# Operands of both token sets beside the classic gate slices, an own bank for some last products, and a later second mixture split

## The chip, the cores and the metric

The kernel runs on one core of a Trainium2 chip. The metric is the device time of one execution in microseconds, as the median of several runs. The profile is that of one further execution, whose own time stands beside its span below. The engines are TensorE (PE in the profile; its weight loads are PEld), VectorE (DVE), ScalarE (ACT), GpSimd (POOL) and SyncE (SP); SP and POOL issue most of the transfers.

## The reference, cut to what matters

One decoder layer for 1024 prompt tokens and 8 sample tokens that share the weights (1032 tokens, model width 1024, feed-forward width 2816), all in float32:

```python
h = rmsnorm(x, g_attn_norm)
z = h @ w_in                       # q, k, v of both branches, mLSTM gates, merge gates A and M
y_a = sliding_window_attention(...) @ w_att_out
y_m = mlstm_chunkwise(...) @ w_mlstm_out
mixed = sigmoid(gate_a) * y_a + sigmoid(gate_m) * y_m
x = x + mixed @ w_out
h2 = rmsnorm(x, g_ffn_norm)
x = x + (silu(h2 @ w_gate) * (h2 @ w_up)) @ w_down
y = rmsnorm(x, g_final)
```

It also returns the key and value windows and the mLSTM states. gate_a and gate_m are 1024 columns each of `w_in`.

## The kernel before

**Number format.** Every large product is made of three float32r matmuls. Each operand x is split into a high part (an ACT copy to float32r) and a low part (VectorE: x minus the high part), and a product is low weights by high activations, high weights by low activations, and high by high. So each operand costs one ACT and one VectorE instruction before TensorE can use it.

**Classic slices and products of seven.** Part of the matrix products are done in the classic way, one weight slice of 128 columns after the other (`Slice`, `gemm`). The others, called visits, use Winograd's form of Strassen's scheme: a two by two block product with 7 instead of 8 block products. The weights of a visit form four blocks, from which four sums S1 to S4 are made (`weight_sum`, on VectorE); the activations form four blocks b11, b12, b21, b22, which are turned into sums t1 to t4 once for all visits and split into high (`gh` in the gate stage, `Th` in the feed-forward) and low (`gl`, `Tl`) operands. The tokens are cut into two halves of 516, and each half into two sets of 258. An operand of the activations belongs to one set.

**A visit.** `product(n, sets)` issues product n, for n = 0, 2, 1, 4, 3, 5, 6 in this order. For one set and four blocks of rows in the contraction it is 12 matmuls of 128 by 258. Three PSUM tiles of two banks each are used: product 2 goes to `b`, products 4 and 6 to `d`, and 0, 1, 3 and 5 all go to `a`, one added on top of the other. After each of them ACT copies the state of `a` (p1 after 0, U2 after 1, V after 3), and the next product into `a` has to wait for that copy. Product 6 adds on top of what product 4 left in `d`. `after(n, sets)` gives the work that follows a product: `now` is issued with this step, `later` with the next. Where a visit does both sets at once (24 matmuls a product) product 0 of the next visit stands between products 3 and 5. The first gate visit and the first up visit do set 0 alone and then set 1; for set 0, and in the last visit of a chain, nothing stands between 3 and 5.

**Stages in order of time.** Classic slices up to attention and the mLSTM; four classic gate slices m0, a0, m1, a1 (`gate_tile`, three chunks of 344 tokens each, 12 jobs); six gate visits `GV` (columns 2 to 7); the two branch projections (`branch_tile`, wm and wa); the output projection in 16 tiles (`wo_tile`, 8 for set 0, then 8 for set 1); 22 up visits `UP`; 20 down visits `DOWN`; a classic rest of the down projection and the final norm.

**What runs beside the classic gate slices.** After each of the 12 jobs one entry of the list `gate_work` is issued (`gate_plan`): the rest of the head gate, block sums and operands of set 0 (`GateBlocks(0)`, B0), the weight operands of the first gate visit (`p(0)`, `p(2)`, `p(1)`, `p(4, 3)`) and those of set 1 (B1). Each job's own evacuation, the sigmoid `sg` (L1071), is issued on ACT before that job's entry and behind those of all earlier jobs. The weight operands 0 and 4 use the buffers `wh`, 2 and 3 the buffers `wl`, two of each, which the classic slices use too. What the list leaves is attached to the first steps of the first visit (`first_hooks`, `hk[-1]`, `hk[0]` and so on: hooks of the step of that number).

**What sets the order.** TensorE, SP and POOL run in program order (`IN_ORDER`). ACT and VectorE run in program order for everything issued through `main_line`; other instructions are placed by a scheduler when their inputs are ready. `side.step` lets side jobs (generators) go on beside an output tile: 6 steps for each `wo_tile`, two more at its start. The side jobs of the output stage are the first 6 steps of `residual()` (the transposes of the input rows), then `mix_rest()` (the split of the mixture for set 1), then the rest of `residual()`. `next_split` splits the weight slice that comes two tiles later; in `run` it is issued after a tile's matmuls and before its evacuation.

**Buffers.** `up` has 20 buffers of 1032 columns (U), `tp` 11 smaller ones (T), `vp` 18. PSUM has 8 banks: six are the three two-bank tiles (`ps_d`), in the earlier stages six single ones (`ps_g`, `ps_a`), and two are `ps_t`, for transposes and small sums.

Of the kernel before, what the change touches and what calls it, by code (L numbers as in the profile page):

```python
# [35 lines left out]
HB = 258  # L36
# [48 lines left out]
def decoder_step(ctx, tc, x_prompt, x_sample, cache_k, cache_v, st_c, st_n, st_m, rel_bias, w_in, b_if, sinks,  # L85
# [204 lines left out]


    class Tile:
        def __init__(self, prods, evac, per=0.0, before=None, pre=None, mm=None, after=None):
            self.prods, self.evac, self.per, self.before, self.pre, self.mm, self.after = prods, evac, per, before, pre, mm, after

# [36 lines left out]
    def run(tiles, jobs, sl, loads, splits):  # L332
# [10 lines left out]
        for n, (t, c) in enumerate(jobs):  # L343
            tile_ = tiles[t]
            if t not in started:
                started.add(t)
                if tile_.before:
                    tile_.before()
            if tile_.pre:
                tile_.pre(c)  # L350
            rate = tile_.per / sum(len(rhs) for _, rhs in tile_.prods)

            def tick():
                acc[0] += rate
                if acc[0] >= 1.0 - 1e-9:
                    acc[0] -= 1.0
                    side.step(1)

            pss = []
            for i, (w, rhs) in enumerate(tile_.prods):  # L360
                if tile_.mm:
                    ps = tile_.mm(w, tick)
                else:
                    ps = ps_g(f"{w.name}_{c}")
                    gemm(ps, w.w, rhs, slice(*CHUNKS[c]), tick)
                pss.append(ps)
                if last[t] == n and splits and not w.own:
                    next_split()
            main_line(tile_.evac, c, *pss)
            if tile_.after:  # L370
                tile_.after()
            if n + 2 < FIRST and len(sl) > FIRST and not mark:
                sl[n + 2].split()
            if n + 1 == START and not mark:
                mark.append(len(nc.cur_bb.bb.instructions))
# [827 lines left out]

    def mix_rest():
        for th in range(2):
            for k in range(0, KD, 4):
                mix_split(1, th, range(k, k + 4))
                yield

    d_x1 = [dp.tile([P, NT], F32, name=f"d_x1_{j}") for j in range(KD)]  # L1210
# [174 lines left out]

    ngate = len(tiles)
    tiles.extend(branch_tile(n, j) for n in "ma" for j in range(KD))
    tiles.extend(wo_tile(s, j) for s in range(2) for j in range(KD))


# [100 lines left out]
    class Visit:  # L1491
# [40 lines left out]
                self.ops[n] = o  # L1532

        def view(self, t, sets):
            return t[:, sets[0]:sets[-1] + 1, 0:HB]

        def small(self, name, sets):
            return T(f"{name}{self.name}_{sets[0]}", [P, len(sets), HB])

        def product(self, n, sets):  # L1540
            bank = "b" if n == 2 else "d" if n in (4, 6) else "a"
            first = n in (0, 2, 4)
            if first:
                self.box[bank] = ps_d(f"{bank}{self.name}_{sets[0]}")
            ps, o = self.box[bank], self.ops[n]
            for s in sets:
                for k in range(self.nk):
                    hi, lo = self.act(n, s, k)
                    for i, (a, b) in enumerate(((o[:, 1, k], hi), (o[:, 0, k], lo), (o[:, 0, k], hi))):
                        pe.matmul(ps[:, s, 0:HB], a, b, start=(first and k == 0 and i == 0), stop=(k == self.nk - 1 and i == 2),  # L1550
                                  skip_group_check=not first)

    def prep_rest():
# [4 lines left out]
    class UpVisit(Visit):  # L1558
# [16 lines left out]
        def after(self, n, sets):  # L1575
# [22 lines left out]
                later.append(c22)  # L1598
            elif n == 5:
                box["s2"] = self.small("s2", sets)  # L1600
                now.append(lambda: act.activation(box["s2"], get("a"), AF.Silu))
                later.append(lambda: tt(dve, box["uu"][:, 1, s0:s1], box["uu"][:, 1, s0:s1], box["s2"], ALU.mult))
            elif n == 6:
                u1 = box["uu"][:, 0, s0:s1]
# [7 lines left out]
    class GateVisit(Visit):  # L1612
# [16 lines left out]
        def after(self, n, sets):  # L1629
# [16 lines left out]
            elif n == 3:  # L1646
                box["V"] = self.small("V", sets)
                now.append(lambda: act.copy(box["V"], get("a")))
# [17 lines left out]
    class DownVisit(Visit):  # L1666
# [21 lines left out]
        def after(self, n, sets):  # L1688
# [12 lines left out]
            elif n == 3:  # L1701
                box["V"] = self.small("V", sets)
                now.append(lambda: act.copy(box["V"], get("a")))
# [501 lines left out]
```

## Time and profile before

| what | value |
|---|---|
| median of 3 runs | 1424.61 us (1424.02 to 1426.32) |
| the profiled execution's own time | 1427.2 us |
| its span | 1425.2 us, 26898 instructions |
| PE busy | 1388.3 us (97%) |
| DVE busy | 909.4 us (64%) |
| ACT busy | 620.6 us (44%) |
| POOL busy | 139.5 us (10%) |
| granted TensorE clock, mean | 0.99 |

A row of the timeline holds the start, the duration, the engine, the line and the operation, and what it writes and reads; in square brackets the idle time of the engine before it and what ended it. Successive matmuls overlap, so a matmul that shows 0.28 us follows the last after 0.12. A row of waits holds who waited for whom, the sum, the number and the longest. Names of tiles are cut: ag, bg, dg are the PSUM tiles of the gate visits, af, bf, df those of the up visits, ad, bd, dd those of the down visits, and op0 to op6 the weight operands. Line L124 is the helper for all two-operand VectorE instructions.

### The profile page before, as it was taken

The page shows a single profiled execution, that of the slowest core. Times are in us where ns is not written, and L with a number is a line of the kernel's source. Part 1 is how long each engine was busy: PE and PEld are TensorE (multiplying, and loading weights), DVE is VectorE, ACT ScalarE, POOL GpSimd, SP SyncE. Part 2 cuts the span into 40 slices and gives each one's busy share as a digit, 9 for nine tenths or more (in the row PEclk, how much of TensorE's full clock was granted, in tenths as well). Part 3 has the DMA queues.
Part 4 walks back from the last instruction along what each step waited for, and adds up shares of the span by engine and source line. Part 5 has one row for each costly group of instructions (what it writes and reads, how often), then busy time and mean ns, then how long its engine had stood idle before and what let it go on. Part 6 is the DMA issues. An engine that isn't in the chain of part 4 may idle for free.

```text
span 1425.2 us, 26898 instructions
## 1 busy us (share of the span) xinstructions
PE 1388.3 (97%) x10723; PEld 1350.7 (95%) x10724; DVE 909.4 (64%) x1827; ACT 620.6 (44%) x1403; POOL 139.5 (10%) x240
## 2 busy tenths in 40 slices
PE   8999999999879999999999999999999999999996
PEld 7998888999879999999999999999999999999996
DVE  7252657784664444653776666766666668888875
ACT  6243477654343332354453444434343433333324
POOL 4011011001110110000110111111001100000003
PEclk9999999999989999999999999999999999999999
DMA  7144214013323255588531444443344467777633
GB/s 218 32 126 98 67 55 97 16 60 121 97 77 108 90 215 179 159 287 294 188 104 53 156 164 165 152 146 119 123 132 149 164 202 274 228 249 233 215 119 119
DMA packets 179172, 208.41 MB, mean 146 GB/s; under 512 B 20638, under 2 KB 137634, under 8 KB 179032
## 3 DMA queue, kind: packets, MB, share of 16 engines
q1 hardware_dynamic: 161928, 151.72, 34.8%
q0 software_dynamic: 16688, 54.40, 10.3%
q8 instruction: 84, 1.38, 0.4%
q10 hardware_dynamic: 432, 0.59, 0.1%
q14 instruction: 40, 0.33, 0.1%
HBM read 140.31 MB, written 68.96 MB: 147 GB/s over the span
## 4 chain that ended last, share of the span: by engine, by line
PE 92%; DVE 3%; ACT 1%; DMA 1%; issue 1%; POOL 0%; SPq 0%; POOLq 0%; ACTq 0%; DVEq 0%
PE af L1550 17%; PE df L1550 9%; PE ad L1550 8%; PE wo L1246 7%; PE ag L1550 5%; PE bf L1550 4%; PE dd L1550 4%; PE o L225 3%; PE mv L225 3%; PE wm L1366 3%; PE q L225 3%; PE dg L1550 2%; PE wa L1366 2%; PE bd L1550 2%; PE mk L225 2%; PE mq L225 2%
## 5 line engine op out<-in xcount | busy, mean ns | idle before, releaser
L1550 PE MATMUL af<-Th,op5f 128*128 128x258 f32 x352 | 68.3, 286 | 2.9 <-ACT Vf L1592 2.9
L1550 PE MATMUL df<-Th,op6f 128*128 128x258 f32 x352 | 67.8, 284 | 0.0
L1550 PE MATMUL af<-Th,op3f 128*128 128x258 f32 x352 | 67.5, 284 | 0.0
L1550 PE MATMUL af<-Th,op1f 128*128 128x258 f32 x352 | 67.4, 283 | 0.0
L1550 PE MATMUL af<-Th,op0f 128*128 128x258 f32 x352 | 67.2, 283 | 0.0
L1550 PE MATMUL bf<-Th,op2f 128*128 128x258 f32 x352 | 67.2, 283 | 0.0
L1550 PE MATMUL df<-Th,op4f 128*128 128x258 f32 x352 | 67.1, 283 | 0.0
L1550 PEld LDWEIGHTS af<-Th,op5f 128*128 128x128 f32 x352 | 56.5, 191 | 3.3 <-ACT Vf L1592 3.3
L1586 ACT ACTIVATE s1f<-s1f 128x516 f32<-128x516 f32 (+1 forms) x23 | 14.2, 618 | 101.7 <-DVE s1f L124 101.7
L1550 PEld LDWEIGHTS df<-Th,op6f 128*128 128x128 f32 x352 | 56.5, 191 | 0.0
L1550 PEld LDWEIGHTS af<-Th,op0f 128*128 128x128 f32 x352 | 56.1, 189 | 0.0
L1550 PEld LDWEIGHTS af<-Th,op1f 128*128 128x128 f32 x352 | 55.9, 189 | 0.0
L1550 PEld LDWEIGHTS af<-Th,op3f 128*128 128x128 f32 x352 | 55.9, 189 | 0.0
L1550 PEld LDWEIGHTS bf<-Th,op2f 128*128 128x128 f32 x352 | 55.8, 189 | 0.0
L1550 PEld LDWEIGHTS df<-Th,op4f 128*128 128x128 f32 x352 | 55.8, 189 | 0.0
L1550 PE MATMUL af<-Tl,op1f 128*128 128x258 f32 x176 | 49.8, 283 | 0.6 <-DVE Tl L124 0.6
L1550 PE MATMUL df<-Tl,op6f 128*128 128x258 f32 x176 | 50.0, 284 | 0.0
L1550 PE MATMUL af<-Tl,op5f 128*128 128x258 f32 x176 | 50.0, 284 | 0.0
L1550 PE MATMUL af<-Tl,op0f 128*128 128x258 f32 x176 | 50.0, 284 | 0.0
L1550 PE MATMUL df<-Tl,op4f 128*128 128x258 f32 x176 | 49.7, 282 | 0.0
L1550 PE MATMUL af<-Tl,op3f 128*128 128x258 f32 x176 | 49.7, 282 | 0.0
L1550 PE MATMUL bf<-Tl,op2f 128*128 128x258 f32 x176 | 49.7, 282 | 0.0
(668 smaller groups left out, 4784.0 us busy)
## 6 DMA issues: line engine op xcount, KB each, us to landing
ta<-d_t SPq DMA_DIRECT2D x63, 516.0 KB, 6.5
Yd<-in_w_down_dram SPq DMA_DIRECT2D x40, 256.0 KB, 3.4
d_t<-h POOLq DMA_DIRECT2D x18, 516.0 KB, 4.2
d_t<-t POOLq DMA_DIRECT2D x18, 516.0 KB, 4.8
Xf<-in_w_gate_dram SPq DMA_DIRECT2D x22, 256.0 KB, 4.3
Xf<-in_w_up_dram SPq DMA_DIRECT2D x22, 256.0 KB, 6.9
Yf<-in_w_gate_dram SPq DMA_DIRECT2D x22, 256.0 KB, 3.1
Yf<-in_w_up_dram SPq DMA_DIRECT2D x22, 256.0 KB
```

Of the source, the lines that this page charges most:

```text
L225: pe.matmul(o, a[:, k, :], b[:, cs], start=(k == 0 and i == 0), stop=(k == n - 1 and i == len(passes) - 1))
L1246: pe.matmul(ps[:, th, 0:HB], a[:, k, :], b, start=(k == 0 and i == 0), stop=(k == KD - 1 and i == 2))
L1366: pe.matmul(ps[:, c, 0:CW], a[:, k, :], b[:, cs], start=(k == 0 and q == 0), stop=(k == 3 and q == 2))
L1550: pe.matmul(ps[:, s, 0:HB], a, b, start=(first and k == 0 and i == 0), stop=(k == self.nk - 1 and i == 2), skip_group_check=not first)
L1586: lambda: act.activation(box["s1"], box["s1"], AF.Silu)])
```

## The change

There are three parts.

1. **Order of the gate operands.** The block sums and operands of set 1 (B1) go into `gate_work` directly behind those of set 0. The weight operands 0, 2 and 1 follow them in the entries of the last three jobs, S3 in the last one; operands 4 and 3 move to the hooks of the first two steps of the first visit. Before, the low parts 1, 3 and 6 of set 1, with the high part 6, were in those hooks.
2. **Own bank for some last products.** Where a visit lists a set in `alone`, product 5 goes to a tile `c` of its own instead of on top of `a`: a single bank of `ps_t` for one set, a `ps_d` tile for both. VectorE then adds V and `c` where ACT read `a` before; in the down visit there is one more addition into the result. `alone` is set for both sets of the first up visit, for both sets together in the last down visit and the last gate visit, and for set 0 of the first gate visit.
3. **Mixture.** The last branch tile is evacuated before its `next_split`. `mix_rest` works on two instead of four blocks a step, so 8 steps instead of 4, and is issued through `main_line`.

```diff
     class Tile:
+        evac_first = False
...
-                if last[t] == n and splits and not w.own:
+                if last[t] == n and splits and not w.own and not tile_.evac_first:
                     next_split()
             main_line(tile_.evac, c, *pss)
+            if last[t] == n and splits and tile_.evac_first:
+                next_split()
...
     def mix_rest():
         for th in range(2):
-            for k in range(0, KD, 4):
-                mix_split(1, th, range(k, k + 4))
+            for k in range(0, KD, 2):
+                main_line(mix_split, 1, th, range(k, k + 2))
                 yield
...
     tiles.extend(branch_tile(n, j) for n in "ma" for j in range(KD))
+    tiles[-1].evac_first = True
...
+        alone = ()
+        def apart(self, sets):
+            return sets in self.alone
...
         def product(self, n, sets):
-            bank = "b" if n == 2 else "d" if n in (4, 6) else "a"
-            first = n in (0, 2, 4)
+            bank = "c" if n == 5 and self.apart(sets) else "b" if n == 2 else "d" if n in (4, 6) else "a"
+            first = n in (0, 2, 4) or bank == "c"
             if first:
-                self.box[bank] = ps_d(f"{bank}{self.name}_{sets[0]}")
+                one = bank == "c" and len(sets) == 1
+                self.box[bank] = (ps_t if one else ps_d)(f"{bank}{self.name}_{sets[0]}")
...
# UpVisit.after
             elif n == 5:
                 box["s2"] = self.small("s2", sets)
-                now.append(lambda: act.activation(box["s2"], get("a"), AF.Silu))
+                if self.apart(sets):
+                    now.append(lambda: tt(dve, box["s2"], get("c"), box["V"], ALU.add))
+                    now.append(lambda: act.activation(box["s2"], box["s2"], AF.Silu))
+                else:
+                    now.append(lambda: act.activation(box["s2"], get("a"), AF.Silu))
...
# GateVisit.after
             elif n == 3:
                 box["V"] = self.small("V", sets)
                 now.append(lambda: act.copy(box["V"], get("a")))
-                now.append(lambda: tt(dve, box["V"], get("d"), box["V"], ALU.add))
-                later.append(lambda: out("m", 1, box["V"]))
+                box["c22"] = self.small("c22", sets) if self.apart(sets) else box["V"]
+                now.append(lambda: tt(dve, box["c22"], get("d"), box["V"], ALU.add))
+                later.append(lambda: out("m", 1, box["c22"]))
+            elif n == 5 and self.apart(sets):
+                now.append(lambda: tt(dve, box["V"], get("c"), box["V"], ALU.add))
+                later.append(lambda: out("a", 1, box["V"]))
...
# DownVisit.after
                 later.append(lambda: add(1, 1, get("d")))
+                if self.apart(sets):
+                    later.append(lambda: add(0, 1, box["V"]))
             elif n == 5:
-                now.append(lambda: add(0, 1, get("a")))
+                now.append(lambda: add(0, 1, get("c" if self.apart(sets) else "a")))
...
+    UP[0].alone = (0,), (1,)
+    DOWN[-1].alone = (0, 1),
...
+    GV[0].alone = (0,),
+    GV[-1].alone = (0, 1),
...
# gate_plan, from the seventh entry of gate_work on
-            seq(p(0), lambda: B0.lo(6), p(2)),
-            p(1),
-            p(4, 3),
-            seq(B1.b12, B1.b11, B1.t1),
-            seq(B1.b22, B1.t2, B1.t3, lambda: B1.hi(4)),
-            seq(B1.b21, B1.t4, lambda: B1.hi(1), lambda: B1.lo(4), lambda: B1.hi(3)),
+            seq(lambda: B0.lo(6), B1.b12, B1.b11, B1.t1),
+            seq(B1.b22, B1.t2, B1.t3),
+            seq(B1.b21, lambda: B1.hi(4), B1.t4, lambda: B1.hi(1), lambda: B1.lo(4)),
+            seq(p(0), lambda: B1.hi(3), p(2), lambda: B1.lo(1)),
+            seq(p(1), lambda: B1.hi(6), lambda: B1.lo(3)),
+            seq(lambda: B1.lo(6), lambda: g.weight_sum(3)),
         ])
         hk = {j: [] for j in range(-1, 7)}
-        hk[-1].append(ml(seq(lambda: B1.lo(1), lambda: B1.hi(6), lambda: B1.lo(3))))
-        hk[0].append(ml(seq(lambda: B1.lo(6))))
+        hk[-1].append(ml(p(4)))
+        hk[0].append(ml(p(3)))
         hk[1].append(ml(p(5)))
```

More of the change, by code (lines that the diff above doesn't have):

```diff
@@ L1534, in view @@
         def view(self, t, sets):
-            return t[:, sets[0]:sets[-1] + 1, 0:HB]
+            return t[:, :, 0:HB] if t.shape[1] == len(sets) else t[:, sets[0]:sets[-1] + 1, 0:HB]
+        alone = ()
+        def apart(self, sets):
+            return sets in self.alone
         def small(self, name, sets):
@@ L1540, in product @@
         def product(self, n, sets):
-            bank = "b" if n == 2 else "d" if n in (4, 6) else "a"
-            first = n in (0, 2, 4)
+            bank = "c" if n == 5 and self.apart(sets) else "b" if n == 2 else "d" if n in (4, 6) else "a"
+            first = n in (0, 2, 4) or bank == "c"
             if first:
-                self.box[bank] = ps_d(f"{bank}{self.name}_{sets[0]}")
+                one = bank == "c" and len(sets) == 1
+                self.box[bank] = (ps_t if one else ps_d)(f"{bank}{self.name}_{sets[0]}")
+                if one:
+                    self.box[bank] = self.box[bank].rearrange("p (a c) -> p a c", a=1)
             ps, o = self.box[bank], self.ops[n]
@@ L1549, in product @@
                     for i, (a, b) in enumerate(((o[:, 1, k], hi), (o[:, 0, k], lo), (o[:, 0, k], hi))):
-                        pe.matmul(ps[:, s, 0:HB], a, b, start=(first and k == 0 and i == 0), stop=(k == self.nk - 1 and i == 2),
+                        pe.matmul(ps[:, s if ps.shape[1] > 1 else 0, 0:HB], a, b, start=(first and k == 0 and i == 0), stop=(k == self.nk - 1 and i == 2),
                                   skip_group_check=not first)
```

## The prediction

> **What bounds the kernel now.** I read the chain of waits first, then the list of what TensorE waited for, then each place in the timeline.
>
> ```profile
> PE 92%; DVE 3%; ACT 1%; DMA 1%; issue 1%; POOL 0%; SPq 0%; POOLq 0%; ACTq 0%; DVEq 0%
> PE ag L1550 <- ACT sg L1071: 10.6, 1, 10.6
> PE af L1550 <- ACT Vf L1592: 2.9, 2, 2.4
> ```
>
> TensorE carries 92% of the chain, and the change takes no matmul away. It can only win the holes in TensorE's time. The largest is at the start of the gate visits.
>
> ```profile
> 397.12 1.06 ACT L1137 ACTIVATE gh<-gbb 128x1032 fp32r<-128x1032 f32 x1 [7.26 <-DVE gbb L124]
> 398.09 0.44 ACT L1071 ACTIVATE sg<-ga 128x344 f32<-128x344 f32 x1
> 387.67 0.32 PE L225 MATMUL ga<-hh,wh_ga 128*128 128x344 f32 x1
> 398.58 0.58 PE L1550 MATMUL ag<-hh,op0g 128*128 128x258 f32 x1 [10.60 <-ACT sg L1071]
> 412.16 0.29 PE L1550 MATMUL ag<-hh,op0g 128*128 128x258 f32 x1
> ```
>
> TensorE issues the last classic gate matmul at 387.67 and the first product at 398.58. That product reuses the bank that the last classic sigmoid (sg) reads. The sigmoid is short, but it stands on ACT behind a conversion (gh) of the second set, which waits 7.26 us for VectorE's block sums. The second cost of the hole is the clock.
>
> ```profile
> 397.89:401.31 3.42, 2.73 (x12) 0.50 0.13 52
> 749.46:752.88 3.42, 1.03 (x8) 0.99 0.50 145
> 752.88:756.29 3.41, 3.41 (x18) 0.51 0.00 0
> 131.66:135.07 3.41, 1.68 (x13) 1.00 0.99 189
> ```
>
> These windows (length, TensorE busy, count, granted clock, DMA) are 3.41 us long. In the hole the clock has fallen to half, and is so still when TensorE is back (397.89). A window with 1.03 busy has a half-clock window behind it, one with 1.68 doesn't.
>
> **The gate operands.** From 387.67 to 412.16, where the second set begins, lie 24.49 us: 7 products of 12 matmuls.
>
> ```profile
> 409.19 0.39 PE L1550 MATMUL ag<-hh,op5g 128*128 128x258 f32 x1 [0.46 <-ACT Vg L1648]
> 370.65:388.00 17.35, 17.34 (x110) 17.05 (x109) 5.11 (x8) 2.48 (x5) 1.08 (x2) 1.00 0.09 33
> 388.00:404.10 16.10, 5.52 (x25) 5.52 (x26) 15.29 (x14) 6.49 (x10) 1.62 (x3) 0.59 0.09 33
> L124 DVE TENSOR_TENSOR gl<-gbb,gh 128x1032 fp32r<-128x1032 f32 x5 | 6.1, 1228 | 0.0
> L124 DVE TENSOR_TENSOR op4g<-S3g,op4g 128x512 fp32r<-128x512 f32 x1 | 0.7, 693 | 5.6 <-ACT op4g L1529 5.6
> 376.68 0.63 ACT L1529 ACTIVATE op0g<-Xg 128x512 fp32r<-128x512 f32 x1 [7.05 <-PE gm L225]
> 405.34 0.64 ACT L1529 ACTIVATE op5g<-S4g 128x512 fp32r<-128x512 f32 x1 [3.39 <-DVE S4g L124]
> 406.18 0.35 ACT L1645 COPY U2g<-ag 128x258 f32<-128x258 f32 x1
> ```
>
> Two products took 412.16 - 409.19 = 2.97 us at full clock, restart included, so one is 1.45 and seven are 10.1 us. With no hole the stretch is 0.16 (one classic matmul) + 10.1 = 10.3, and 24.5 - 10.3 = 14.2 us is the most that can be won. Can VectorE be ready? The work that the change regroups lies between 370.65 and 404.10, with 5.11 + 15.29 = 20.4 us of VectorE time (third busy column). Until 388.00, 17.35 us are under classic matmuls. Before, VectorE idled in 12 of them: the weight operand op0 came first and waited 7.05 us on ACT for a buffer that the classic slice m1 still read, then op4 5.6 us for that of a1, and the block sums stood behind both. In the new order the block sums need no buffer of a slice, op0 and op2 are asked for when m1 has ended (before 376.68), and op4 when a1 has. So VectorE runs through and ends at about 370.65 + 20.4 = 391.1; what is left at 388 is the last low part (1.23 us) and S3, op4 and op3 (0.69 each). None of these is needed by the first two products. Step by step, with 1.23 for a block operation, 0.69 for a weight operation, 1.06 and 0.64 for their ACT halves: op1's high half ends on ACT at 387.3 and gh6 at 388.3, so the last sg runs to 388.7, and the first product starts at 388.7 and not at 387.83: 0.9 left. The product n=1 adds into the bank that ACT copies p1 from; that copy now stands behind op4's high half, which needs S3 (391.0): copy at 391.55 to 391.95 against 391.6, 0.4 left. The product n=3 waits for the copy of U2 (0.35), which now stands behind op5's high half and a sigmoid: 395.4 against 394.95, 0.6 left with the restart. The wait in the row of 409.19 is gone: the last product has its own bank, one of the two single ones that nothing else uses in this stage, and V's copy is needed only by VectorE. The second set then starts at 387.83 + 10.1 + 1.9 = 399.9: **12.2 us** won. Bounds: 14.2 if VectorE's and ACT's lag is nowhere seen, 9.3 if each of four products (0, 1, 4, 3) waits for one block operation (4 x 1.23 = 4.9 in place of 1.9).
>
> SP: the next visit's load waits for the last block buffer, free with the last low part, 404.1 before and about 390.4 then, still 9 us before the second set begins. No other load or store changes its place.
>
> **The last gate visit.**
>
> ```profile
> 517.34 0.28 PE L1550 MATMUL ag<-gh,op3g 128*128 128x258 f32 x1
> 518.29 0.39 PE L1550 MATMUL ag<-hh,op5g 128*128 128x258 f32 x1 [0.68 <-ACT Vg L1648]
> 523.13 2.38 DVE L124 TENSOR_TENSOR yml<-hb,ymh 128x1032 fp32r<-128x1032 f32 x2 [1.51 <-ACT ymh L230]
> 518.27 0.70 DVE L124 TENSOR_TENSOR Vg<-dg,Vg 128x516 f32<-128x516 f32 x1 [4.56 <-ACT Vg L1648]
> ```
>
> Start to start 0.95 instead of 1.45/12 = 0.12, and the matmul after the wait takes 0.39 instead of 0.28: 0.94 lost. A wait shown as x thus costs x + 0.26. The own bank takes the buffer of the second product, read long before. VectorE gets one more addition (0.70) beside the splitting of the branch operands (yml), in front of which it idles 1.51 us, and these hide it; without that cover the branch would start up to 0.7 late. I take **0.9** (0.2 to 0.95).
>
> **The first up visit.** This one I cost at almost nothing, though its waits are 2.9 us.
>
> ```profile
> 745.60 0.39 PE L1550 MATMUL af<-Tl,op1f 128*128 128x258 f32 x1 [0.60 <-DVE Tl L124]
> 752.04 0.36 ACT L1592 COPY Vf<-af 128x258 f32<-128x258 f32 x1
> 752.45 0.39 PE L1550 MATMUL af<-Th,op5f 128*128 128x258 f32 x1 [2.39 <-ACT Vf L1592]
> 752.16 1.23 DVE L124 TENSOR_TENSOR Tl<-xg,Th 128x1032 fp32r<-128x1032 f32 x1 [1.19 <-ACT Th L1459]
> 753.32 0.42 DVE L124 TENSOR_TENSOR uu<-df,Vf 128x258 f32<-128x258 f32 x1
> 754.98 0.69 DVE L124 TENSOR_TENSOR op2f<-Yf,op2f 128x512 fp32r<-128x512 f32 x1
> 756.93 0.28 PE L1550 MATMUL bf<-Th,op2f 128*128 128x258 f32 x1
> 736.20:743.00 6.80, 6.80 (x58) 6.80 (x58) 6.67 (x10) 1.09 (x4) 0.00 (x0) 1.00 0.00 0
> ```
>
> For set 0 the wait of 0.46 goes, but VectorE, busy 6.67 of 6.80 us here, gets the addition c+V (0.42, as uu) in a chain that ends in Tl, for which TensorE waits at 745.60. With the silu now behind it, I take this chain as 0.55 later, and so do all the steps to 754.98. For set 1, product 5 no longer waits for V and runs some 2 us earlier. But product 6 writes the bank d that c22 (uu<-df,Vf) reads, and c22 stands behind the last Tl on VectorE: 753.32 + 0.42 + 0.55 = 754.3. The hole of 2.39 moves from before product 5 to before product 6, which ends at 755.8. The next visit's product 2 needs op2's low half, 754.98 + 0.69 + 0.55 + 0.34 for the second c+V = 756.6, against 756.93: **0.2** won. Bounds: +4.9 if the additions cost nothing and both waits go (2.9 and 2 x 0.26) with the half clock (1.5, below), -1.3 if the half clock stays.
>
> **The last down visit.**
>
> ```profile
> 1378.27 1.72 PE L1550 MATMUL ad<-ta,op5d 128*128 128x258 f32 x12 [0.68 <-ACT Vd L1703]
> 1379.82 1.70 PE L1550 MATMUL dd<-ta,op6d 128*128 128x258 f32 x12
> 1379.05 0.70 DVE L124 TENSOR_TENSOR x<-dd,x 128x516 f32<-128x516 f32 x1
> ```
>
> Product 5 can start at 1378.27 - 0.68 - 0.15 = 1377.4, but product 6 overwrites the bank that VectorE reads until 1379.75, and that read follows V's copy as before. So product 6 starts where it did: **0**. The added addition (0.70) lies in the time before product 6 ends. Bounds -0.7 and +0.95.
>
> **The mixture split.**
>
> ```profile
> 615.77 1.29 DVE L124 TENSOR_TENSOR wl_wo<-ws_wo,wh_wo 128x512 fp32r<-128x512 f32 x2
> 616.98 0.87 DVE L124 TENSOR_TENSOR sga<-wa,sga 128x688 f32<-128x688 f32 x1
> 619.92 0.39 PE L1246 MATMUL wo<-mh,wl_wo 128*128 128x258 f32 x1 [0.43 <-ACT mh L230]
> ```
>
> The last branch tile's evacuation (616.98) stands behind a weight split of two operations (1.29) on VectorE, which the next output tile needs only later. Evacuated first, and without the second set's splits in its way, it ends over 1.3 us earlier, and the wait goes with its restart: 0.7, and 0.2 for the low half that followed. I take **0.9** (0 to 1.4). The second set's splits then lie in the first two output tiles; their four added steps push the later residual transposes by as many steps, without adding one.
>
> **Sum.** 12.2 + 0.9 + 0.2 + 0 + 0.9 = 14.2 us. The profiled execution took 1427.2 (span 1425.2) and becomes 1413.0; it stands 2.6 above the median, 1424.6, so **1410.4**.
>
> **Rivals.**
>
> *Late gate operands.* VectorE doesn't run through, and four products wait as bounded above: 9.3 for 12.2, so 1413.3, and 1414.2 with the 0.9 on the last sg doubled as well. For it: 20.4 us of work have 17.35 of cover. Against: the first two products need none of the rest.
>
> *The half clock stays in the first up visit.* The moved hole is 2.3 us, so a window has at least 1.1 busy, between 1.03 (halved) and 1.68 (not). A half-clock window of 3.41 us does the work of 1.9 and loses 1.5, of which 0.2 hide: 1410.4 + 1.3 = 1411.7. The rows put it at a third or less. [...]
>
> *All holes go.* Halfway between what I take and the upper bounds: 13.2 + 0.9 + 2.6 + 0.5 + 1.1 = 18.3, so 1406.3. For it: where VectorE has slack, the own bank takes the wait away whole. Against: it has none at 736.
>
> *Slower: the output tiles' buffers.*
>
> ```profile
> 631.62 0.63 ACT L230 ACTIVATE wh_wo<-ws_wo 128x512 fp32r<-128x512 f32 x1 [0.80 <-PE wo L1246]
> 639.87 0.63 ACT L230 ACTIVATE wh_wo<-ws_wo 128x512 fp32r<-128x512 f32 x1 [0.80 <-PE wo L1246]
> ```
>
> Ten of the eleven `t` buffers hold residual rows. With four more steps ahead of them, the squares of output tiles 1 and 2 find a buffer only in the middle of the next tile; the weight split of the tile after stands behind them on ACT. A tile takes 8.25 us (639.87 - 631.62). If the split slips by a whole tile both times, TensorE loses 16.5 and two half-clock windows, 3.0: 1429.9. It decides once 14.2 us are lost, 1.7 tiles; I count a lag of half a tile, for which nothing waits.
>
> *The hole only changes its name.* The scheduler or another reader of the bank keeps TensorE at 398: 1424.
>
> **Chances.** Forecast 0.55, late operands 0.15, half clock 0.12, all holes 0.10, unchanged 0.05, slower 0.03. 1406 to 1416 holds the forecast, the half clock, late operands and most of all holes, some 0.85. 0.2% is 2.8 us, about what a measurement of this kernel can tell from none: faster 0.92, within 0.05, slower 0.03.
>
> **What would show it.** The wait for sg falls from 10.6 to about 1 and no window from 380 to 400 has half the clock; small waits for the copies of p1 and U2 appear; no wait for Vg; in the up visit the wait is before op6 and not op5; in the last down visit it is before op6d; none before wo. A wait of over 3 us in the gate stage, or a wo row waiting for a split, would make the prediction wrong.

## The result, and the profile after

The changed kernel took 1410.71 us in the median (1408.66 to 1411.56, 4 runs), the kernel before beside it 1425.22 (1424.02 to 1426.32): 14.5 us less, a ratio of 0.9896 with a 95% interval of 0.9879 to 0.9913. The forecast was 1410.4, 14.2 less. The profiled execution took 1411.56 us, 15.6 less than that of before, with a span of 1409.7 us.

The chain of waits of the changed kernel, by engine:

```profile
PE 93%; DVE 2%; DMA 2%; ACT 1%; issue 1%; POOL 0%; SPq 0%; POOLq 0%; ACTq 0%; DVEq 0%
```

What TensorE waited for around the edits (us in total, times, the longest):

```profile
PE df L1563 <- DVE uu L124: 1.5, 1, 1.5
PE af L1563 <- DVE Tl L124: 0.9, 1, 0.9
PE af L1563 <- ACT Th L1463: 0.8, 1, 0.8
PE dd L1563 <- DVE x L124: 0.8, 1, 0.8
PE ag L1563 <- ACT sg L1074: 0.6, 1, 0.6
PE bf L1563 <- DVE op2f L124: 0.6, 1, 0.6
PE ag L1563 <- ACT U2g L1662: 0.3, 1, 0.3
```

The 10.6 us for sg are 0.6, the rows for Vg and wo are gone, and in the first up visit the 2.9 us for Vf have become 1.5 for uu (product 6) and 0.6 for op2f, with 0.8 for Th and 0.9 for Tl where Tl alone had 0.6. To see what each place gave, I measure between starts of TensorE rows, since what lies ahead of 380 us differs between executions of any of these kernels (the last classic gate matmul started anywhere from 385.21 to 388.88). Of the kernel before (its rows of 387.67 and 412.16 stand in the prediction):

```profile
524.18 0.32 PE L1366 MATMUL wm<-ymh,wl_wm 128*128 128x344 f32 x1
615.64 0.36 PE L1246 MATMUL wo<-mh,wl_wo 128*128 128x258 f32 x1
725.03 0.28 PE L1550 MATMUL af<-Th,op0f 128*128 128x258 f32 x1
759.81 0.28 PE L1550 MATMUL af<-Th,op1f 128*128 128x258 f32 x1
1172.52 0.52 PE L1550 MATMUL ad<-ta,op0d 128*128 128x258 f32 x3
1382.30 0.50 PE L225 MATMUL fl<-tu,wl_wl 128*128 128x512 f32 x1 [0.79 <-DVE x L124]
```

And of the changed kernel:

```profile
387.62 0.32 PE L225 MATMUL ga<-hh,wh_ga 128*128 128x344 f32 x1
388.55 0.39 PE L1563 MATMUL ag<-hh,op0g 128*128 128x258 f32 x1 [0.61 <-ACT sg L1074]
399.70 0.29 PE L1563 MATMUL ag<-hh,op0g 128*128 128x258 f32 x1
510.73 0.32 PE L1369 MATMUL wm<-ymh,wl_wm 128*128 128x344 f32 x1
602.43 0.37 PE L1249 MATMUL wo<-mh,wl_wo 128*128 128x258 f32 x1
710.60 0.28 PE L1563 MATMUL af<-Th,op0f 128*128 128x258 f32 x1
745.89 0.28 PE L1563 MATMUL af<-Th,op1f 128*128 128x258 f32 x1
1158.40 0.53 PE L1563 MATMUL ad<-ta,op0d 128*128 128x258 f32 x3
1365.43 1.69 PE L1563 MATMUL dd<-ta,op6d 128*128 128x258 f32 x12 [0.77 <-DVE x L124]
1366.96 0.39 PE L225 MATMUL fl<-tu,wl_wl 128*128 128x512 f32 x1
```

Five stretches hold the edits: **G**, last classic gate matmul (387.67, 387.62) to the second set's first product (412.16, 399.70); **L**, from there to wm; **M**, wo to the first up product; **U**, that product to the second up visit's first product of op1; **D**, first down product to fl. The same rows of every profile below give this table; a star is a window of half clock inside the stretch, and "against before" is the median less that of the kernel before in the same group of runs.

| kernel | G | L | M | U | D | median | against before |
|---|---|---|---|---|---|---|---|
| before | 24.49* | 112.02 | 109.39* | 34.78* | 209.78 | 1425.22 | |
| changed | 12.08 | 111.03 | 108.17* | 35.29* | 208.56 | 1410.71 | -14.5 |
| gate order only | 12.82 | 112.00 | 108.11 | 34.82* | 209.62 | 1412.93 | -11.2 |
| old gate order | 23.13* | 111.07 | 106.54 | 34.59 | 208.92 | 1420.05 | -4.1 |
| no own bank, up | 12.10 | 111.03 | 106.64 | 34.83* | 208.67 | 1409.53 | -14.6 |
| no own bank, last down | 12.09 | 111.03 | 106.65 | 36.65** | 208.56 | 1410.99 | -13.1 |
| before, hole filled | 23.84 | 112.03 | 107.93 | 34.79* | 209.78 | 1425.95 | +1.9 |
| old evacuation | 12.08 | 111.03 | 109.20* | 34.59 | 208.58 | 1409.93 | -14.1 |
| old mixture split | 12.10 | 111.03 | 106.97 | 35.65* | 208.72 | 1409.23 | -14.8 |
| no own bank, last gate | 12.10 | 112.00 | 106.65 | 34.60 | 209.62 | 1411.19 | -12.8 |
| changed, again | 12.10 | 111.03 | 108.16* | 36.65** | 208.56 | 1411.46 | -14.0 |
| gate and down edits | 12.17 | 110.98 | 108.15* | 36.95** | 207.85 | 1409.87 | -15.6 |
| up order | 12.17 | 110.98 | 108.15* | 32.88* | 207.75 | 1406.16 | -19.3 |
| up order with GpSimd | 12.16 | 110.98 | 108.09* | 32.41 | 207.61 | 1406.79 | -18.7 |

Between the two first rows: G 12.4 less, L 1.0, M 1.2, U 0.5 more, D 1.2 less. The stars matter when it is read: between kernels whose code for the stretch is the same, M differs by 1.5 and U by up to 2.4, and the changed kernel's own two profiles have U at 35.29 and 36.65. Each row is one profile, and D moves by up to 0.4 with edits that lie far ahead of it (208.56 to 208.92), so smaller differences there are not read. The medians are too coarse for the small terms: without the up visit's own banks, with the old evacuation or with the old split they are 14.1 to 14.8 below the kernel before, and the changed kernel's two are 14.0 and 14.5 below.

### The profile page after: what moved, and what is told of

Read it like the earlier page. It is cut to its first block, busy times and chain, and to the rows that moved or that the text cites. A ratio compares the mean times of both kernels' runs of the same rounds, so it can differ in the third digit from the quotient of the medians.

```text
span 1409.7 us, 26898 instructions
## 1 busy us (share of the span) xinstructions
PE 1385.0 (98%) x10723; PEld 1347.9 (96%) x10724; DVE 912.3 (65%) x1832; ACT 620.3 (44%) x1403; POOL 139.2 (10%) x240
## 3 DMA queue, kind: packets, MB, share of 16 engines
q1 hardware_dynamic: 161928, 151.72, 34.8%
## 4 chain that ended last, share of the span: by engine, by line
PE 93%; DVE 2%; DMA 2%; ACT 1%; issue 1%; POOL 0%; SPq 0%; POOLq 0%; ACTq 0%; DVEq 0%
PE af L1563 17%; PE df L1563 9%; PE ad L1563 8%; PE wo L1249 7%; PE bf L1563 4%; PE ag L1563 4%; PE dd L1563 4%; PE o L225 3%; PE mv L225 3%; PE wm L1369 3%; PE wa L1369 3%; PE q L225 3%; PE dg L1563 2%; PE bd L1563 2%; PE mk L225 2%; PE mq L225 2%
## 5 line engine op out<-in xcount | busy, mean ns | idle before, releaser
L1563 PE MATMUL af<-Th,op5f 128*128 128x258 f32 x336 | 64.1, 283 | 0.0
L1599 ACT ACTIVATE s1f<-s1f 128x516 f32<-128x516 f32 (+1 forms) x23 | 14.2, 618 | 103.3 <-DVE s1f L124 103.3
L1563 PEld LDWEIGHTS af<-Th,op5f 128*128 128x128 f32 x336 | 53.4, 189 | 0.0
```

Source lines behind the costliest of these rows:

```text
L1563: pe.matmul(ps[:, s if ps.shape[1] > 1 else 0, 0:HB], a, b, start=(first and k == 0 and i == 0), stop=(k == self.nk - 1 and i == 2), skip_ ...
L1599: lambda: act.activation(box["s1"], box["s1"], AF.Silu)])
```

## The experiments

**The gate order alone** (the kernel before with the new `gate_plan` and nothing else):

```
-            seq(p(0), lambda: B0.lo(6), p(2)),
...
+            seq(p(0), lambda: B1.hi(3), p(2), lambda: B1.lo(1)),
...
-        hk[-1].append(ml(seq(lambda: B1.lo(1), lambda: B1.hi(6), lambda: B1.lo(3))))
+        hk[-1].append(ml(p(4)))
```

> The kernel before, with one edit of the change alone: the new order of the gate operands. My theory, that the order by itself earns the gate term and the own bank only the small wait behind it: the wait for sg falls from 10.6 us to about 0.6, no window at 390 to 405 has half the clock, a wait for Vg of about 0.5 us stays, and the second set's first gate product starts 12.46 - 0.46 - 0.26 = 11.7 us earlier than before, at about 400.4 us; the time is 11.7 below the kernel before. Rival, that the order needs the own bank, since V's copy now stands behind more work on ACT: the wait for Vg grows to 1.5 us or more, and the second set's first product starts at 401.5 or later.

G fell from 24.49 to 12.82, by 11.67 where 11.7 was expected, the median by 11.2 (ratio 0.9922, 0.9906 to 0.9939). V's wait stays as it was, in the timeline of this kernel:

```profile
395.05 0.39 PE L1550 MATMUL ag<-hh,op5g 128*128 128x258 f32 x1 [0.46 <-ACT Vg L1648]
```

So the order by itself earns 11.7 of the gate's 12.4, and the own bank adds 12.82 - 12.08 = 0.74. The rival falls.

**The changed kernel with the old gate order** (the same lines the other way round):

> The changed kernel with the old order of the gate operands. My theory: the wait for sg is 10.6 us again and the half clock is back at 390 to 405; of the first gate visit's gain only the own bank's 0.7 stays, so that the second set's first product starts at about 411.4 us, and the time is 11.7 above the changed kernel's. Rival, that the own bank does more (by a bank that the waiting first product no longer needs): the wait for sg is under 10 us.

The wait for sg is 10.6 again and the half clock is back from 392 to 402. G is 23.13, 11.05 more than in the changed kernel and not 11.7. The median is 4.1 below the kernel before, so 9.9 to 10.4 above the changed kernel's in place of 11.7. With the old order the own bank gave 24.49 - 23.13 = 1.36 and not 0.7. Behind this hole the clock was full again 4.2 us after the first product (402.31 against 398.11), in the kernel before 6.05 us after it (404.63 against 398.58), so part of the other 0.6 may be the clock's; no run splits it.

**The first up visit without own banks**:

```
-    UP[0].alone = (0,), (1,)
```

> The changed kernel without the own banks of the first up visit. My theory, that they lose there because their additions delay a chain on VectorE: from the up visit's first product to the second up visit's product of op2 it takes 31.9 us as before, and not 32.3 as in the changed kernel; the time is 0.4 below the changed kernel's; the wait for the copy of Vf before op5 is 2.4 us again, the waits of 0.8 for Th and of 0.9 for Tl before op1 shrink to the 0.6 of before, and the wait for uu before op6 is gone. Rival, the prediction's +0.2: the stretch is 32.1 us or more in this kernel than it takes with the own banks; rival of full gain: 2 us or more above.

As expected: the wait for Vf is back (2.9 us in two), those for uu, op2f and Th are gone, and the stretch to the second up visit's product of op2 is 31.93 against 32.29. But the sign is not a property of the program. U without own banks is 34.78 to 34.83 in all four profiles that have none, with one half-clock window each. With own banks and this order of operands it is 34.59 to 34.60 where the clock stays full, and 35.29 to 36.95 with one or two half-clock windows. Two views of the clock in the up visit, by its own windows of 3.41 us (length, TensorE busy, count, granted clock, the last two of DMA), first of the changed kernel:

```profile
728.90:732.31 3.41, 1.75 (x12) 1.00 0.00 0
732.31:735.72 3.41, 3.41 (x18) 0.50 0.05 13
739.14:742.55 3.41, 1.70 (x13) 1.00 0.00 0
```

and of the same program run again, in the last group below:

```profile
726.80:730.21 3.41, 1.79 (x12) 1.00 0.00 0
730.21:733.62 3.41, 3.41 (x17) 0.50 0.02 6
737.04:740.45 3.41, 1.63 (x14) 1.00 0.00 0
740.45:743.86 3.41, 3.14 (x15) 0.50 0.00 0
```

The grid of windows falls differently over the same holes in each execution. The hole before op1 (0.8 for Th, then 0.9 for Tl) and the one before op6 (1.5 to 2.3 for uu) leave 1.75 and 1.79, and 1.70 and 1.63 us busy in the windows of these two profiles, and half clock followed all but the one with 1.70 (more of this in the last section).

**The last down visit without its own bank**:

```
-    DOWN[-1].alone = (0, 1),
```

> The changed kernel without the own bank of the last down visit. My theory, that the 0.95 us at the end come from the bank that the first fl tile falls on, which the extra bank of the last gate visit has moved, and not from the last down visit's own bank: the wait of 0.7 for Vd before op5 is back, the wait before op6 is gone, fl still has no wait, and from the first product of the down visits to the end it takes the same as in the changed kernel within 0.3 us. Rival, that the own bank earned it: fl waits 0.8 for x again, and that stretch is 0.9 to 1.0 us longer.

D is 208.56 in both. The wait only changes its name, as the prediction had it (0.68 for Vd before op5, none before op6):

```profile
1362.43 1.72 PE L1563 MATMUL ad<-ta,op5d 128*128 128x258 f32 x12 [0.68 <-ACT Vd L1724]
1365.49 0.39 PE L225 MATMUL fl<-tu,wl_wl 128*128 128x512 f32 x1
```

And fl has no wait without that bank either: the 1.2 us of D don't come from this edit.

**The kernel before with the hole filled**: 46 matmuls of zeros ahead of the first gate product.

```
+        wps = ps_t("warm")
+        for i in range(46):
+            pe.matmul(wps, wz[:, 0:P], wz, start=True, stop=True)
```

> The kernel before, with 46 matmuls of zeros (128x128 by 128x512, into a bank that nothing reads) added ahead of the first gate product, so that TensorE is busy in most of the hole while the operands are as late as before; nothing of the result changes. It measures by itself what the clock took of the hole. My theory, that the first two products ran at half clock only because TensorE stood idle: no window from 390 to 405 has half the clock, the first product starts at 398 to 399 as before, and the stretch from it to the second set's first product falls from 13.6 us to about 11.0 (seven products of 1.45 and the waits of about 0.9 for Vg and others); the time is 2.6 below the kernel before. Rival, that VectorE, not the clock, sets the pace of these products: the clock is full, but the stretch stays at 13 us or more, with longer waits between the products. If the clock falls to half even so, it does not follow the idle time.

The stretch from 390 to 405 ran at full clock:

```profile
390.00:405.00 15.00, 14.34 (x84) 8.94 (x83) 14.90 (x14) 5.62 (x9) 1.61 (x3) 1.00 0.10 35
399.80 0.39 PE L1550 MATMUL ag<-hh,op0g 128*128 128x258 f32 x1 [0.66 <-ACT sg L1071]
407.57 0.39 PE L1550 MATMUL ag<-gh,op3g 128*128 128x258 f32 x1 [1.47 <-ACT U2g L1645]
```

My theory falls. From the first product to the second set it took 12.92 us against 13.58: with operands this late the clock was worth 0.66, not 2.6. The rival's longer wait came, and its stretch of 13 or more was missed by 0.08. VectorE, busy 14.90 of these 15 us (third busy column), sets the pace once TensorE is fast enough, and a wait of 1.47 for U2 appears that half clock had hidden. The median rose all the same, by 1.9 (ratio 1.0010, 1.0001 to 1.0019). Only 1.0 of it lies between first and last instruction (the runs' spans have medians of 1423.0 and 1422.0); the rest lies outside what the profile covers. No stretch of the table is longer; this profile has a half-clock window at 135 us, ahead of all of them, that the profile of the kernel before has not, and whether the other runs had it stays open. Taken in this order of steps, the gate gain splits: the hole 10.91 to 0.93 (10.0), half clock 0.66, the products' operands in time 12.92 - 11.89 = 1.03 (the 11.89 from the gate order alone, the part of its G that lies behind the first product), the own bank 0.74.

**The old evacuation**:

```
-    tiles[-1].evac_first = True
```

> The changed kernel with the last branch tile's evacuation behind the weight split again, as before; the second set's mixture splits stay later. Stretch: from the first output matmul to the first up product, which took 106.6 us in the three profiles of the changed kernel and its variants that had no half clock in it, and 108.1 with neither of the two mixture edits. My theory, that the evacuation put first earns most of the 1.5 us: the wait of wo for mh is about 0.4 or longer again and the stretch is 107.3 or more. Rival, that the later splits earn it: no wait before wo, and the stretch is 106.9 or less.

A wait is back, for the low half of the same operand:

```profile
605.65 0.39 PE L1249 MATMUL wo<-ml,wh_wo 128*128 128x258 f32 x1 [0.48 <-DVE ml L124]
```

M is 109.20 with a half-clock window, 1.0 above the changed kernel's 108.17 with one. Less the 1.5 us that such a window costs in M (108.17 against 106.65) that is an estimate of 107.7, where 107.3 or more was expected.

**The old mixture split**:

```
-            for k in range(0, KD, 2):
-                main_line(mix_split, 1, th, range(k, k + 2))
+            for k in range(0, KD, 4):
+                mix_split(1, th, range(k, k + 4))
```

> The changed kernel with the second set's mixture splits where they were, four at a time; the evacuation stays ahead of the weight split. Theory as in the experiment before it: the wait of wo is gone or under 0.3 us, and the stretch from the first output matmul to the first up product is 106.6 to 107.0. Rival, that the later splits are needed as well: a wait of 0.3 us or more before wo, the stretch 107.3 or more.

No wait before wo, M 106.97. The two edits together earn 1.3 to 1.5 us, both ends without half clock in M (107.93 with the hole filled and 108.11 with the gate order alone, neither with a mixture edit, to 106.65). Of this the evacuation earns 1.0 and the later splits 0.3.

**The last gate visit without its own bank**:

```
-    GV[-1].alone = (0, 1),
```

> The changed kernel without the own bank of the last gate visit; the last down visit keeps its own. My theory, that this one edit earns two things, the last gate visit's 1.0 us and, by the place of the banks, the last 0.95 us before fl: the wait of 0.7 for Vg is back, and the stretch from the second set's first product to the first wm matmul is 112.0 us as before in place of 111.0; the bank that the last down product fills is the first fl tile's again, fl waits 0.8 for x, and the stretch from the first down product to the first fl matmul is 209.5 to 209.8 in place of 208.6; the time is 2.0 above the changed kernel's. Rival, that the two have nothing to do with one another: 112.0, but fl has no wait, and the time is 1.0 above.

```profile
505.11 0.39 PE L1563 MATMUL ag<-hh,op5g 128*128 128x258 f32 x1 [0.68 <-ACT Vg L1665]
1365.79 0.50 PE L225 MATMUL fl<-tu,wl_wl 128*128 128x512 f32 x1 [0.79 <-DVE x L124]
```

Both waits are back, 860 us apart: L is 112.00 and D 209.62. The three double banks are handed out again as they come free, and one more of them in the last gate visit changes which bank later tiles get. By the addresses in the built programs, the first fl tile lies in bank 2 in every one; the last d, which VectorE reads last of all, lies in banks 2 and 3 before and without this line, and in 6 and 7 with it, where the last a, read earlier, has 2 and 3. One line of this change is worth 1.0 + 1.1 us, and its median, 12.8 below the kernel before in place of 14.0 to 14.5, says the same within the runs' spread.

**The changed kernel again, and three candidates to beat it**, on one chip.

> The changed kernel once more, as it is, beside the next three on the same chip. Theory: the stretches that hold no half clock repeat to 0.1 us (last classic gate matmul to the second set's first product 12.1, second set to wm 111.0, first down product to fl 208.6). The first up visit's differs between executions: from its first product to the second up visit's product of op1 34.6 us if no window has half the clock there and 35.3 or more if one has. Rival, that the visit's length belongs to the program: 35.3 again, with half the clock at the same place.

G, L and D repeat to 0.02 us and M to 0.01; U came out at 36.65 with two half-clock windows. The rival falls: the visit's length is not fixed by the program.

The gate and down edits:

```
-            seq(p(1), lambda: B1.hi(6), lambda: B1.lo(3)),
-            seq(lambda: B1.lo(6), lambda: g.weight_sum(3)),
+            seq(p(1), lambda: g.weight_sum(3)),
+            lambda: B1.lo(3),
...
+            elif n == 4 and self.apart(sets):
+                now.append(lambda: add(1, 1, get("d")))
```

> The changed kernel with two more edits, a candidate to beat it: the conversion ahead of the last sigmoid and the low part behind it come after the first two products, with the sum S3 ahead; and in the last down visit the bank that product 6 overwrites is read when product 4 has ended, in place of after V's copy. My theory: the waits for sg (0.6) and for p1 and U2 go and the last classic gate matmul to the second set's first product takes 10.5 to 11.0 us in place of 12.1; the wait of 0.8 before op6 in the last down visit goes and the stretch to fl is 207.6 in place of 208.6; together 2.0 to 2.6 below the changed kernel. Rival, that the deferred operands or the loads behind them come late: a new wait at the second set's first products or for a load, and less than 1.2 below.

The gate part was wrong: G is 12.17, none of the 1.1 to 1.6 expected. In its timeline the last classic matmul starts at 386.64, the sigmoid with nothing ahead of it right behind, and the first product still waits:

```profile
387.05 0.46 ACT L1074 ACTIVATE sg<-ga 128x344 f32<-128x344 f32 x1 [0.82 <-PE ga L225]
387.56 0.39 PE L1563 MATMUL ag<-hh,op0g 128*128 128x258 f32 x1 [0.60 <-ACT sg L1074]
394.36 0.39 PE L1563 MATMUL ag<-gh,op3g 128*128 128x258 f32 x1 [0.76 <-ACT U2g L1662]
```

The 0.6 is the evacuation itself, and the low part moved behind the products made U2's wait 0.76 in place of 0.31. The down part held: no wait before op6, D 0.7 less (1.0 expected).

The up order, in addition to these:

```
-                (2, (lambda: B.hi(5), lambda: B.lo(5), B.t4)), (3, (lambda: B.hi(6), lambda: B.lo(6)))]
+                (2, (lambda: B.hi(5), B.t4, lambda: B.lo(5))), (3, (lambda: B.hi(6), lambda: B.lo(6))), (5, (prep_rest,))]
```

> As the kernel before this one, and in the first up visit the subtraction t4 goes ahead of the low part of block 5, and op2's low part ahead of the sums for op1. My theory, that the second half of the visit's waits comes from the order on VectorE, not from too much work: the waits of 1.5 before op6 and of 0.6 before op2 go, those of 0.8 and 0.9 before op1 stay; the up stretch is 32.5 to 33 us without and 33 to 34 with a half clock, some 2 below. Rival, that VectorE has no slack there: the waits only move to another operand, and the stretch is 34 or more.

The waits before op6 and op2 are gone, those before op1 stay, and U is 32.88 with one half-clock window, where 33 to 34 was expected. The median is 1406.16, against 1409.87 for the kernel before this one and 1411.46 for the changed kernel beside it; the ratio to before is 0.9864 (0.9848 to 0.9881). This version beats both kernels. So these two waits came from the order on VectorE: two steps put forward, none taken away.

The up order with the subtraction t4 on GpSimd:

```
-            tt(dve, self.b21, self.b21, self.t2_, ALU.subtract)
+            tt(pool if self.s else dve, self.b21, self.b21, self.t2_, ALU.subtract)
...
-        hook(6, B.t2, B.t3)
+        hook(6, B.t2, lambda: B.hi(1), B.t4, B.t3, lambda: B.lo(1), lambda: B.hi(4))
```

> As the second kernel of this group, and in the first up visit the second set's operands in another order: the high parts of blocks 1 and 4 and the low part of 1 at the end of the first set's visit, ahead of the s1 of the second set, and t4 on GpSimd in place of VectorE (an estimate of 2.5 us, from the 1.28 us that GpSimd takes for 128x512), so that VectorE has 1.15 us less to do. My theory: all four waits of the visit in the changed kernel (0.8, 0.9, 1.5, 0.6) shrink to under 0.5 in all, no window there has half the clock, and the up stretch is 31.0 to 31.8 us; with the gate and the down edits 5 below the changed kernel. Rival, that VectorE is full and the low parts come late all the same: waits for Tl of over 1 us in all, 33 or more.

No half clock, but U is 32.41 and not 31.0 to 31.8, and a wait of 1.6 for Tl is left. The median, 1406.79, can't be told from the version before it. The reason is in the last section.

## Why the prediction held, point by point

The time was 0.3 us from the forecast. The gate term, by far the largest, came by the steps that were forecast; two small terms were off by about a microsecond with opposite signs, which is luck.

- **Gate operands**, 12.2 forecast, 12.46 measured between the starts of the second set (412.16 to 399.70), 12.41 as G. The steps held. VectorE ran through: it was busy for 16.25 of the last 17.35 us under classic matmuls, against 5.11 before (third busy column below), and S3 ended at 390.81 (forecast 391.0). sg left 0.77 behind the classic matmul's 0.16 (forecast 0.9). p1's copy cost 0.37 (the first matmul of op1 starts 0.38 behind the one before it in place of 0.12, and takes 0.11 longer; forecast 0.4), and U2's wait of 0.31 cost 0.58 by the same reckoning (forecast 0.6). Vg's wait went, and no window from 380 to 400 had half the clock. Of the changed kernel:

```profile
390.13 0.68 DVE L124 TENSOR_TENSOR S3g<-Xg 128x512 f32<-128x512 f32 x1
387.11 1.05 ACT L1140 ACTIVATE gh<-gbb 128x1032 fp32r<-128x1032 f32 x1
388.06 0.43 ACT L1074 ACTIVATE sg<-ga 128x344 f32<-128x344 f32 x1
391.79 0.39 PE L1563 MATMUL ag<-gh,op1g 128*128 128x258 f32 x1
395.28 0.39 PE L1563 MATMUL ag<-gh,op3g 128*128 128x258 f32 x1 [0.31 <-ACT U2g L1662]
370.60:387.95 17.35, 17.34 (x111) 17.05 (x109) 16.25 (x18) 7.12 (x11) 2.16 (x4) 1.00 0.15 53
```

  The products take 1.45 only when their operands are there: with the hole filled and the old order, the seven took 12.92 at full clock and not 10.1.
- **Last gate visit**, 0.9 forecast, 1.0 measured (L).
- **First up visit**, 0.2 forecast. The step that failed is that the half clock goes: the wait did move from before product 5 to before product 6, but TensorE also waited for Th and Tl in a row before op1, which the forecast had as one small delay of 0.55. In three of the eight profiles with own banks and this order the clock stays full and U is 0.2 less. The waits are longer there too, 4.6 us in all against 3.5 before (Vf 2.9, Tl 0.6); what brings the visit out ahead is that it has no half-clock window (worth 1.5 us in M). In five U is 0.5 to 2.2 more, and the mean of the eight, 35.6, is 0.8 above the 34.8 without. The rival with the half clock, given 0.12, is the commoner case. The forecast's own numbers, 756.6 against 756.93 at the second visit's product of op2, differ by 0.33 and not by the 0.2 taken; where the clock stays full that stretch is 31.6 against 31.9, 0.3 less. Single holes of 1.8 to 2.4 us (waits for uu and Vf), and two of 0.7 to 0.8 and 0.9 in a row (Th, then Tl), were followed by half clock in some of the profiles.
- **Last down visit**, 0 forecast for its own bank and 0 measured for it. What the forecast missed is D's 1.2 us, from the other end of the kernel: the last gate visit's extra bank moved the place of the last d. The step that failed is "the own bank takes the buffer of the second product", which stopped at that visit and did not follow where the pool's order goes from there.
- **Mixture split**, 0.9 forecast, 1.3 measured where no half clock disturbs it, 1.2 between the two profiles. The forecast had one term for both edits (0.7 for the wait and 0.2 for the low half); apart, the evacuation measured 1.0 and the later splits 0.3.
- **Sum**, 14.2 forecast, 14.5 in the medians. The five stretches give 12.4 + 1.0 + 1.2 - 0.5 + 1.2 = 15.3 of the 15.6 between the profiled executions. The 1.2 missed at the end is partly taken back by the 0.7 too much in the up visit: the total was better than its parts.

Of the other slower rivals, neither the late gate operands nor the output tiles' buffers came. ACT did stand idle for 0.97 and 0.98 us before the squares of output tiles 1 and 2, until the transposes of residual rows ahead of them were done, and TensorE had no wait for it; the half tile of lag that the prediction counted covers it.

## What to carry to other kernels

Here a hole whose operands were late was won by the order on the engine that makes them, and hardly by a bank (0.74) or a faster TensorE (0.66): VectorE does the same work with little idle in it, and later two steps put forward in the up visit brought U from a mean of 35.6 us to 32.9. When a change allocates one more buffer from a rotating pool, follow the pool to its end, since a wait far behind may appear or go (here 0.79 us before fl, 860 us later). Before a microsecond is believed, see if the stretch holds a half-clock window in one of the two profiles (1.5 us in M here).

## What the runs showed of the hardware

**Half clock came in windows on a grid.** In these profiles half-clock stretches began and ended on a grid of 3.41 us whose place differs between executions; in the kernel before they began at 390.98 and 752.79, 106 windows of 3.413 us apart. Windows at full clock in which TensorE was busy for little of the time were followed by one at half clock: with one single hole in them, those with up to 1.63 us busy were followed so and those with 1.65 and more were not (with two holes in one window, 1.75 and 1.79 were, 2.03 was not). The highest of the one kind stands above, of the changed kernel run again; the lowest of the other is, in its first profile:

```profile
131.60:135.01 3.41, 1.65 (x13) 1.00 0.58 210
135.01:138.42 3.41, 3.41 (x28) 1.00 0.84 265
```

So a window that was nearly half busy (1.63 of 3.41) was followed by half clock here. Of windows that were themselves at half clock, those with 2.64 and 2.90 us busy (the kernel before at 397.80, the gate and down edits at 740.30) had another half-clock window behind them; the one with 3.00 (the filled hole at 135.09) had not.

**Half clock behind a fully busy window.** In M the half clock came behind windows that the profile shows as fully busy. The windows and the first and last of the reductions in the changed kernel:

```profile
664.05:667.46 3.41, 3.41 (x36) 1.00 0.99 241
667.46:670.87 3.41, 3.41 (x18) 0.50 0.97 392
664.14 0.28 PE L1412 MATMUL rs<-cst,ssq 128*128 128x1 f32 x2
666.23 0.19 PE L1412 MATMUL rs<-cst,sq 128*2 128x1 f32 x2
```

The first set's sums of squares (`rr_sums`) are 2.27 us of matmuls with a single moving column (664.14 to 666.42). In the seven profiles in which at least 2.07 of these 2.27 us fall into one window, half clock followed; in the other seven, in which the grid splits them (2.02 at most in one window), it didn't. That fits all 14 profiles. My reading, that these matmuls count for less than their time, was tested by no kernel. Even by it they can't count for nothing: two of the windows without half clock behind them held 1.86 and 2.02 us of them, which leaves 1.55 and 1.39 of other work, less than the 1.63 above. Where the half clock came it cost 1.5 us (108.17 against 106.65).

**A VectorE operation beside one on GpSimd.** In the last kernel of the table t4 on GpSimd and a low part on VectorE overlap:

```profile
725.86 3.18 POOL L124 TENSOR_TENSOR xg<-xg,t 128x1032 f32<-128x1032 f32 x1 [10.92 <-PE bf L1563]
726.78 3.35 DVE L124 TENSOR_TENSOR Tl<-t,Th 128x1032 fp32r<-128x1032 f32 x1
730.73 1.22 DVE L124 TENSOR_TENSOR Tl<-xg,Th 128x1032 fp32r<-128x1032 f32 x1
```

A subtraction of this shape takes 1.22 us alone and 3.35 beside GpSimd's, and it ends at 730.13, 1.09 after GpSimd's end at 729.04, as if it had only begun then. In the profiles of the kernel before and of the changed kernel no VectorE operation with two inputs of this size takes over 1.24 us. So 1.15 us taken off VectorE cost it 2.1 (3.35 - 1.22). This is one pair of operations, and why the one waited the trace does not show.
